# A hybrid decoder layer on one core: the order of the opening stage rearranged

## The chip, the core and the metric

The kernel runs on one core of a Trainium2 chip. TensorE (PE), VectorE (DVE), ScalarE (ACT), GpSimd (POOL) and SyncE (SP) each run their own instruction stream in order, and transfers run on 16 DMA engines beside them. The metric is the device time of one execution in microseconds (us); lower is better.

## The reference

One decoder layer for a sequence of 2048 rows of width 1024. Two attention mixers share one normalised, modulated input and one input projection:

```python
mod = jax.nn.silu(c) @ w_ada + b_ada
shift, scale, gate = jnp.split(mod, 3, axis=-1)
h = rms_norm(x, g_pre) * (1.0 + scale[:, None, :]) + shift[:, None, :]
proj = h @ w_in
qa, ka, va, fa, za, qb, kb, vb, zb = jnp.split(proj, split_points, axis=-1)
oa = forgetting_attention(qa, ka, va, fa + b_fgate)        # causal, 8 heads of 64
oa = oa * jax.nn.silu(za)
qb = rope(qb, positions); kb = rope(kb, positions)
ob = sliding_window_sink_attention(qb, kb, vb, sinks)      # window 128, 8 query heads, 2 key heads
ob = ob * jax.nn.silu(zb)
y = jnp.concatenate([oa, ob], axis=-1) @ w_out
x = x + gate[:, None, :] * rms_norm(y, g_post)
```

All inputs and the output are float32 in DRAM.

## The kernel before

Matrix products are made of three float16 products: each operand is split into a high and a low part. Rows are worked on in four chunks of 512 (`CH`); the model dimension is eight tiles of 128 (`KT`). Stages follow each other: the opening stage (lines 421 to 642), the sliding-window branch with the rest of the projections (1041 to 1105), the forgetting attention (1467 to 1555), and the output projection.

**The opening stage.** The rows of `w_ada` come as tiles `wa[half, k]` of 512 KB by `load_ada`; half 1 is `scale`, half 0 is `shift`. `mod` is a sum over the eight k: `ada_pe` lets PE multiply a tile by the broadcast silu(c), `ada_dve` accumulates a tile into `acc` on DVE, `ada_sum` lets PE add `acc` over the partitions, and `ada_col` brings the result from rows to columns. Between them DVE computes the rotary angles (`ang`, lines 510 to 541) from `posi` and `ifr`. x comes in tiles of 128 rows by `load_x`: tiles 0 to 3 and 8 to 11 go through four buffers of the pool `xin`, tiles 4 to 7 lie in the memory of `hT[3]`, tiles 12 to 15 in the pool `xlate`. `squares(ci)` (ACT, line 372) sums the squares of the four tiles of chunk `ci`, `root(ci)` (DVE, 92 to 106, thirteen small instructions) gives the reciprocal root, `normal(ci)` (382 on ACT, 384 on DVE) multiplies the rows by it.

The columns of scale and shift together with a bound on h give `Gp` and `Shp` (624, 625). `turn(ci, k)` transposes one 128-column tile of a chunk on PE (390); its `scaled` applies `Gp` and `Shp` on ACT (396), and its `split` makes the high and low halves of h^T on DVE (400, 401). The weights of kb, vb and zb0 are loaded by `w_load`, and then take `w_scale` (small DVE steps), `w_high` (ACT, 245) and `w_low` (DVE, 251). Their largest elements, which `w_scale` needs, are found by a reduce on DVE and spread over the partitions by PE (569 and 582 for kb and vb; `z_row` and `z_all`, 928 and 932, for zb0).

**The projection units.** After that, the work of PE is a list of units, `punits`, written out by hand. A unit is an eighth of one projection of one chunk (3 matmuls of 512 columns for kb and zb, 12 of 136 columns for vb): eight units for kb (307), eight for vb (740) and eight for zb0 (307) in each of the chunks 0 to 2, with the eight turns of the next chunk put between them at the places in `at_`. `fill` goes through the list; before unit n it calls what `events[n]` holds (`at_slice`), and `tick2` runs what `after(n, f)` has put off by n ticks, one tick every second unit. Other weights go through the same seven steps at fixed distances ahead of their first unit (the `lead` numbers in `add`): a fetch, a reduce, a store and a broadcast through DRAM on POOL's queue, scale, high, low. `spread(g)` copies the cosines and sines to all heads by SP's queue, and `gates` handles the forget gates, with the prefix sums in `sums`.

Within each of the two blocks that call `tc.manual_schedule()` every engine's instructions keep the written order; the two blocks themselves are merged when the program is built (`z_row`'s reduce on DVE, of the second block, runs ahead of `root(1)`, of the first). At run time no order changes.

Line 205 issues `w_load`'s transfers, 365 those of `load_x`, 435 those of `load_ada`, 415 and 416 those of `spread`.

## Time and profile before

| | |
|---|---|
| median of three runs | 1220.21 us (1219.88 to 1220.71) |
| the profiled execution | 1225.81 us, of which its trace spans 1224.0 us |
| mean granted clock of PE | 0.984 |
| busy in the span: PE, DVE, ACT, POOL | 1164.7, 908.5, 674.1, 141.5 us |
| instructions: PE, DVE, ACT, POOL | 10832, 2268, 1117, 252 |

Times inside the text are microseconds from the start of the trace's span. Rows of the timeline give start, duration, engine, line, operation, output and inputs, shapes and count; the bracket gives the idle time of the engine just before and what ended it. `PEld` is PE's weight load, `SPq` and `POOLq` are the instructions that issue transfers.

### The profile page before, as it was taken

To read this page: it belongs to the slowest core of one execution; us is meant where nothing else is said; L and a number is where in the kernel's file an instruction comes from. 1 tells how busy PE (TensorE), PEld (TensorE's weight loads), DVE (VectorE), ACT (ScalarE), POOL (GpSimd) and SP (SyncE) were. 2 spreads that over 40 slices of the span, in tenths; PEclk is the share of its full clock that TensorE was granted. 3 is DMA by queue.
4 is the path that set the end of the run, shared out by engine and by line. 5 is a ranking of instruction groups with operands and counts; after the bars stand their busy time and mean duration, and the time that the engine had idled before them with its cause. 6 is when DMAs were issued, how large, how long until landed. Compare 5 with 4: busy or idle time off the path is not lost.

```text
span 1224.0 us, 27391 instructions
## 1 busy us (share of the span) xinstructions
PE 1164.7 (95%) x10832; PEld 696.0 (57%) x10832; DVE 908.5 (74%) x2268; ACT 674.1 (55%) x1117; POOL 141.5 (12%) x252
## 2 busy tenths in 40 slices
PE   6789999999999998999999999999999979999996
PEld 2457546865558965555555555555555545555553
DVE  6866568586776646688888798878978788676665
ACT  2666445454655541576667666666766769433231
POOL 2011133223232210001010110010000000000000
PEclk9899999999999999999999999999999989999999
DMA  9554332324223322313344323122111146446652
GB/s 324 187 145 138 83 93 75 84 62 103 86 76 80 54 60 44 79 51 92 73 69 77 92 60 77 40 71 48 38 46 42 41 134 193 139 157 192 193 171 84
DMA packets 88180, 120.97 MB, mean 99 GB/s; under 512 B 27852, under 2 KB 63732, under 8 KB 88052
## 3 DMA queue, kind: packets, MB, share of 16 engines
q1 hardware_dynamic: 77076, 86.20, 23.9%
q0 software_dynamic: 10976, 33.03, 11.7%
q8 instruction: 85, 1.39, 0.6%
q14 instruction: 43, 0.35, 0.1%
HBM read 71.82 MB, written 25.18 MB: 79 GB/s over the span
## 4 chain that ended last, share of the span: by engine, by line
PE 78%; DVE 8%; DMA 6%; issue 3%; ACT 3%; SPq 2%; POOL 1%; DVEq 0%; ACTq 0%; POOLq 0%
PE bk L307 29%; PE bk L1405 13%; PE bk L325 7%; PE sta L1256 5%; PE sta L1257 4%; PE bk L1207 4%; PE poa L1282 2%; PE poa L1283 2%; PE poa L1280 2%; PE pxb L864 2%; PE pss L831 2%; PE pob L883 2%; PE bk L1368 1%; DVE pha L1270 1%; DMA hT<-in_x_dram 1%
## 5 line engine op out<-in xcount | busy, mean ns | idle before, releaser
L1263 ACT ACTIVATE p<-sta,lift,scl_qk 128x1024 f32<-128x1024 f32 (+2 forms) x160 | 171.8, 1074 | 132.2 <-PE sta L1257 75.7
L307 PE MATMUL bk<-hT,wh_qk 128*128 128x512 f16 x768 | 196.2, 381 | 0.4 <-DVE a_m L1210 0.4
L1405 PE MATMUL bk<-wohl,oz 128*128 128x512 f16 x768 | 172.1, 379 | 0.0
L1270 DVE TENSOR_TENSOR pha<-p,pha 128x1024 f16<-128x1024 f32 (+2 forms) x160 | 169.2, 1057 | 0.2 <-ACT pha L1267 0.2
L1210 DVE TENSOR_REDUCE a_m<-bk 128x1 f32<-128x512 f32 x192 | 130.4, 686 | 52.3 <-PE bk L1207 51.6
L1267 ACT ACTIVATE pha<-p 128x1024 f16<-128x1024 f32 (+2 forms) x160 | 148.0, 925 | 5.7 <-PE bk L307 0.5
L1405 PEld LDWEIGHTS <-oz 128*128 128x128 f16 x768 | 74.5, 99 | 81.2 <-DVE oz L1392 0.3
L1256 PE MATMUL sta<-T 128*128 128x512 f16 (+1 forms) x320 | 112.3, 351 | 7.4 <-ACT p L1263 7.3
L1280 PE MATMUL poa<-vt,pha 128*128 128x65 f16 x1088 | 117.7, 194 | 1.0 <-DVE ona L1289 1.0
L1283 PE MATMUL poa<-vt,pha 128*128 128x65 f16 x1088 | 117.3, 193 | 1.1 <-DVE pha L1270 1.0
L1282 PE MATMUL poa<-vt,pha 128*128 128x64 f16 x1088 | 117.7, 195 | 0.0
L307 PEld LDWEIGHTS <-wh_qk 128*128 128x128 f16 x768 | 72.7, 98 | 76.2 <-issue 2.9
L1207 PE MATMUL bk<-T 66*128 66x512 f16 (+2 forms) x320 | 110.5, 352 | 3.5 <-DMA T<-stq 3.1
L1280 PEld LDWEIGHTS <-pha 128*128 128x128 f16 x1088 | 102.3, 97 | 15.9 <-DVE ona L1289 2.4
L1257 PE MATMUL sta<-T 69*128 69x512 f16 (+1 forms) x320 | 111.1, 352 | 0.0
L1282 PEld LDWEIGHTS <-pha 128*128 128x128 f16 x1088 | 101.7, 98 | 11.6 <-issue 0.2
L1283 PEld LDWEIGHTS <-pha 128*128 128x128 f16 x1088 | 101.6, 99 | 1.3 <-DVE pha L1270 1.3
L307 PE MATMUL bk<-hT,wh_za 128*128 128x512 f16 x384 | 99.8, 378 | 0.0
L325 PE MATMUL bk<-wh_va,hT 128*128 128x128 f16 x1536 | 91.0, 219 | 1.3 <-issue 1.3
L325 PEld LDWEIGHTS <-hT 128*128 128x128 f16 x1536 | 87.4, 98 | 6.4 <-issue 3.8
L307 PE MATMUL bk<-hT,wh_zb 128*128 128x512 f16 x384 | 89.9, 379 | 1.1 <-DVE wh_zb L251 1.1
L307 PE MATMUL bk<-hT,wh_qb 128*128 128x512 f16 x384 | 87.2, 379 | 0.0
(491 smaller groups left out, 1885.2 us busy)
## 6 DMA issues: line engine op xcount, KB each, us to landing
wa<-in_w_ada_dram SPq DMA_DIRECT2D x16, 512.0 KB
z_d<-tz POOLq DMA_DIRECT2D x32, 256.0 KB, 3.9
T<-stq SPq DMA_DIRECT2D x128, 64.0 KB
T<-o_d SPq DMA_DIRECT2D x16, 512.0 KB
T<-z_d SPq DMA_DIRECT2D x16, 512.0 KB
xr<-in_x_dram SPq DMA_DIRECT2D x16, 512.0 KB
out_dram<-yg SPq DMA_DIRECT2D x15, 512.0 KB
xt<-in_x_dram SPq DMA_DIRECT2D x12, 512.0 KB
```

The source lines that it names most:

```text
L307: PE.matmul(ps, whl[:, a, k, :], hT[ci][:, b, k, :], start=(k == 0 and n == 0), stop=(k == KT - 1 and n == 2))
L325: PE.matmul(ps[:, u * P:(u + 1) * P], hT[ci][:, a, k, u * P:(u + 1) * P], whl[:, b, k, :], start=(k == 0 and n == 0), stop=(k == KT - 1 an ...
L1207: PE.matmul(mx[:, :w], T[0:XM, 0, i * P:(i + 1) * P], T[0:XM, 2, pc * CH:pc * CH + w], start=True, stop=True)
L1256: PE.matmul(self.st[:, o:o + w], T[:, 3, kb_], T[:, 1, qc], start=True, stop=False)
L1257: PE.matmul(self.st[:, o:o + w], T[0:XR, 2, kb_], T[0:XR, 0, qc], start=False, stop=not diag)
L1263: A.activation(self.p32[:, :self.w], self.st[:, :self.w], AF.Exp, scale=scl[f"qk{self.hd}"][:], bias=lift[:])
L1267: A.activation(self.ph[:, 0, :self.w], self.p32[:, :self.w], AF.Copy)
L1270: V.tensor_tensor(self.ph[:, 1, :self.w], self.p32[:, :self.w], self.ph[:, 0, :self.w], op=ALU.subtract)
L1280: PE.matmul(po[:, u, :], ph[:, 0, pq], vt[:, b, hd, 0:65], start=(self.first and n == 0 and u == 0), stop=False)
L1282: PE.matmul(po[:, u, 0:64], ph[:, 0, pq], vt[:, b, hd, 65:VW], start=False, stop=False)
L1283: PE.matmul(po[:, u, :], ph[:, 1, pq], vt[:, b, hd, 0:65], start=False, stop=(self.last and n == len(self.blocks) - 1))
L1405: PE.matmul(py, self.hl[:, i, k, :], w_slot(8 * j + k)[:, cc], start=(k == 0 and m_ == 0), stop=(k == KT - 1 and m_ == 2))
```

## The change

- The positions and `ifr` are loaded by ScalarE's queue, `ifr` first; SP then issues the eight tiles of scale's half of `w_ada` one after the other.
- The early fetch of zb0 on GpSimd's queue goes; the later one by SP stays and follows x 4 to 7.
- The two partial sums `ada_dve(0, 4)` and `(0, 6)`, and root(0) and normal(0), come after the scales of kb and vb; PE's last `ada_pe(0, 7)` goes ahead of the closing sum.
- `w_high("vb")` moves ahead of normal(0), `w_low` of kb and vb and the reduce over zb0 move later.
- normal(1) runs on DVE alone.
- x 8 to 11 are loaded at the end of the opening stage, x 12 to 15 at unit 1.
- squares, root and normal of chunks 2 and 3 come one chunk earlier; the turns lie at other units.
- zb0's steps move among units 10 to 16; the later weights' last steps are one unit earlier; `sums` is three ticks later.

```diff
--- before.py
+++ after.py
@@ -378,7 +378,7 @@
     def normal(ci, us=range(4)):
         for u in us:
             t, r = ci * 4 + u, rstd[ci][1][:, u:u + 1]
-            if ci == 0 or (ci == 1 and u % 2):
+            if ci == 0:
                 A.activation(xt[t], xt[t], AF.Copy, scale=r)
             else:
                 V.tensor_scalar(xt[t], xt[t], r, None, op0=ALU.mult)
@@ -434,16 +434,14 @@
             wa[half, k] = wad.tile([P, D], F32, tag="wa", name=f"wa{half}{k}")
             SP.dma_start(wa[half, k][:], w_ada0[k * P:(k + 1) * P, half * D:(half + 1) * D])
 
-        for k in range(1):
-            load_ada(1, k)
-
+
+        A.dma_start(ifr[:], inv_freq)
         for g in range(4):
-            SP.dma_start(posi[32 * g:32 * g + 32, :], positions[0, g * CH:(g + 1) * CH].partition_broadcast(32))
-        SP.dma_start(ifr[:], inv_freq)
-        for k in range(1, KT):
+            A.dma_start(posi[32 * g:32 * g + 32, :], positions[0, g * CH:(g + 1) * CH].partition_broadcast(32))
+        for k in range(KT):
             load_ada(1, k)
         make_identity(nc, ident)
-        for key in first:
+        for key in first[:2]:
             w_load(key, pieces(key))
         G.dma_start(snk[:], sinks[0].partition_broadcast(P))
         G.dma_start(bfg[:], b_fgate[0].partition_broadcast(P))
@@ -556,53 +554,50 @@
             load_x(t)
         for k in range(3, KT):
             load_ada(0, k)
-        w_load("zb0", pieces("zb0"), SP)
         for t in range(4, 8):
             load_x(t)
+        w_load("zb0", pieces("zb0"), SP)
         ada_sum(1, True)
 
         mx3 = st.tile([P, 2], F32, name="mx3")
         for n, key in enumerate(first[:2]):
             V.tensor_reduce(mx3[:, n:n + 1], wq[key][0][:], axis=AX.XY, op=ALU.max, apply_absolute_value=True)
+        PE.transpose(bk[0][0:2, 0:P], mx3[:], ident[:])
         ada_pe(0, 0, True)
-        ada_pe(0, 3)
-        PE.transpose(bk[0][0:2, 0:P], mx3[:], ident[:])
-        ada_pe(0, 5)
         ada_dve(0, 1, True)
         ada_dve(0, 2, False)
-        squares(0)
-        scl0 = col8("scl0")
-        ada_col(1, scl0)
-        root(0)
-        normal(0)
         m3 = st.tile([2, 1], F32, name="m3")
         V.tensor_reduce(m3[:], bk[0][0:2, 0:P], axis=AX.X, op=ALU.max)
         dg3 = st.tile([2, 2], F32, name="dg3")
         V.tensor_scalar(dg3[:], ident[0:2, 0:2], m3[:], None, op0=ALU.mult)
         PE.matmul(bk[0][:, P:P + 2], ones[0:2, :], dg3[:], start=True, stop=True)
-        ada_dve(0, 4, False)
-        ada_dve(0, 6, False)
-
-        for n in range(2):
-            nn = slice(n * CH, (n + 1) * CH)
-            PE.matmul(pm[0][n][:], ones[:], acc[0][:, nn], start=False, stop=False)
-            PE.matmul(pm[0][n][:], silb[:, KT - 1, :], wa[0, KT - 1][:, nn], start=False, stop=True)
+        ada_pe(0, 3)
+        ada_pe(0, 5)
+        squares(0)
+        scl0 = col8("scl0")
+        ada_col(1, scl0)
         V.tensor_copy(mxs[:, 0:2], bk[0][:, P:P + 2])
         for n, key in enumerate(first[:2]):
             wq[key].append(mxs[:, n:n + 1])
         w_scale("kb")
+        w_scale("vb")
         w_high("kb")
-        w_scale("vb")
-        w_low("kb", 0, 1)
+        w_high("vb")
         scl1 = col8("scl1")
         V.tensor_tensor(scl1[:], scl0[:], cols[:, 24:32], op=ALU.add)
         gcol = col8("gcol")
         V.scalar_tensor_tensor(gcol[:], scl1[:], 1.0, cols[:, 8:16], op0=ALU.add, op1=ALU.mult)
         absg = col8("absg")
         V.scalar_tensor_tensor(absg[:], gcol[:], -1.0, gcol[:], op0=ALU.mult, op1=ALU.max)
+        root(0)
+        normal(0)
+        ada_dve(0, 4, False)
+        ada_dve(0, 6, False)
+        ada_pe(0, KT - 1)
+        ada_sum(0, True)
+        w_low("kb", 0, 1)
         turned = [turn(0, k) for k in range(5)]
         squares(1)
-        w_high("vb")
         shf0 = col8("shf0")
         ada_col(0, shf0)
         shf = col8("shf")
@@ -625,17 +620,19 @@
         V.tensor_scalar(Shp[:], shf[:], ipH[:], 2.0 ** 14, op0=ALU.mult, op1=ALU.mult)
 
         V.tensor_scalar(pfl[:], ipH[:], 0.5, None, op0=ALU.mult)
-        w_low("vb", 0, 1)
         for k in range(KT):
             turned[k][0]()
             turned[k][1]()
             if k == 2:
-                V.tensor_reduce(mxs[:, 2:3], wq["zb0"][0][:], axis=AX.XY, op=ALU.max, apply_absolute_value=True)
+                w_low("vb", 0, 1)
             if k + 5 < KT:
                 turned.append(turn(0, k + 5))
         root(1)
+        V.tensor_reduce(mxs[:, 2:3], wq["zb0"][0][:], axis=AX.XY, op=ALU.max, apply_absolute_value=True)
         normal(1)
         spread(0)
+        for t in range(8, 12):
+            load_x(t)
         for key in ("kb", "vb"):
             kaps[key] = kappa(pws[key], key)
         V.tensor_scalar(kf[:], kaps["vb"][:], PS_SCALE, None, op0=ALU.mult)
@@ -800,7 +797,7 @@
 
         after(1, logs)
         after(3, total)
-        after(4, sums)
+        after(7, sums)
 
     ab = {}
 
@@ -902,11 +899,11 @@
             at = len(punits) - (24 if key[:2] == "za" else 0)
             for n, (lead, f) in enumerate(((42, lambda: w_load(key, pieces(key))), (31, lambda: w_max(key)),
                                            (21, lambda: w_back(key)), (12, lambda: w_scale(key)),
-                                           (8, lambda: w_high(key)), (6, lambda: w_low(key, 0)),
-                                           (4, lambda: w_low(key, 1)), (3, lambda: w_done(key)))):
+                                           (9, lambda: w_high(key)), (7, lambda: w_low(key, 0)),
+                                           (5, lambda: w_low(key, 1)), (4, lambda: w_done(key)))):
                 if key == "zb0":
                     if n >= 3:
-                        events.setdefault(n + 9, []).append(f)
+                        events.setdefault((13, 13, 14, 15, 16)[n - 3], []).append(f)
                 else:
                     events.setdefault(max(at - lead, n), []).append(f)
         if key not in pkeys:
@@ -933,8 +930,9 @@
         V.tensor_copy(mxs[:, 2:3], bk[2][:, P:P + 1])
         wq["zb0"].append(mxs[:, 2:3])
 
-    at_slice(6, z_row)
-    at_slice(10, z_all)
+    at_slice(10, z_row)
+    at_slice(12, z_all)
+    at_slice(1, lambda: [load_x(t) for t in range(12, 16)])
 
     for ci in range(NCH):
         n0 = len(punits)
@@ -944,19 +942,18 @@
             add(*others[ci])
 
             mine, punits[n0:] = punits[n0:], []
-            at_ = [10, 12, 14, 16, 17, 18, 19, 20] if ci else [12, 14, 16, 17, 18, 19, 20, 21]
+            at_ = [6, 8, 10, 12, 14, 16, 18, 20] if ci else [13, 15, 17, 18, 19, 20, 21, 22]
             for n, u in enumerate(mine):
                 punits.append(u)
                 if n in at_:
                     punits.append(lambda ci=ci, k=at_.index(n): turn_x(ci + 1, k))
-            if ci:
+            if ci < 2:
+
                 for u in range(4):
-                    at_slice(n0 - 9 + 2 * u, lambda ci=ci, u=u: squares(ci + 1, (u,)))
-                    at_slice(n0 + 3 + u, lambda ci=ci, u=u: normal(ci + 1, (u,)))
-                at_slice(n0 + 2, lambda ci=ci: root(ci + 1))
+                    at_slice(n0 + (3 if ci else 9) + u, lambda ci=ci, u=u: squares(ci + 2, (u,)))
+                    at_slice(len(punits) - 6 + u, lambda ci=ci, u=u: normal(ci + 2, (u,)))
+                at_slice(len(punits) - 9, lambda ci=ci: root(ci + 2))
             at_slice(n0 + 12, lambda ci=ci: spread(ci + 1))
-            if ci < 2:
-                at_slice(n0 + 12, lambda ci=ci: [load_x(t) for t in range(4 * ci + 8, 4 * ci + 12)])
     n0 = len(punits)
     at_slice(n0, lambda: open_fox())
     at_slice(n0 + 8, gates)
```

## The prediction

> **What bounds the kernel now.** I read the page first, then busy time by stretch (columns: stretch and its length, then busy time and count for PE, PEld, DVE, ACT, POOL, then granted clock, DMA share, GB/s).
>
> ```profile
> PE 1164.7 (95%) x10832; PEld 696.0 (57%) x10832; DVE 908.5 (74%) x2268; ACT 674.1 (55%) x1117; POOL 141.5 (12%) x252
> ...
> 58.40:81.30 22.90, 20.66 (x178) 14.30 (x178) 15.79 (x49) 18.59 (x30) 1.27 (x1) 1.00 0.52 150
> ...
> 103.00:126.50 23.50, 21.80 (x176) 15.61 (x175) 17.86 (x43) 14.11 (x26) 3.61 (x5) 0.93 0.36 90
> ...
> 160.00:300.00 140.00, 140.00 (x1424) 89.15 (x1423) 99.47 (x278) 76.81 (x215) 41.88 (x79) 1.00 0.33 83
> ```
>
> PE is busy 95% of the span, and from 160 to 300 us it has no gap (140.00 of 140.00). The instruction order per engine is fixed at build time, so whatever arrives earlier at 160 us arrives earlier at the end. The change is therefore priced in the first 160 us, where PE has gaps. There are two parts: the adaLN stage, which ends when h^T's factors `Gp`, `Shp` are known, and projection chunks 0 to 2 (kb, vb, zb0 on 512 rows each, with the next chunk's h^T turns between them).
>
> **Term 1: when h^T can start.** Timeline rows (start, duration, what, idle before):
>
> ```profile
> 4.36 0.88 POOL L205 DMA_DIRECT2D wr_zb<-in_w_in_dram  x1
> ...
> 13.38 0.49 DVE L514 TENSOR_SCALAR ang<-ang,ifr 128x512 f32<-128x512 f32 x1 [1.28 <-DMA ifr<-in_freq_dram]
> ...
> 22.24 0.75 DVE L478 TENSOR_SCALAR acc<-wa,sil 128x1024 f32<-128x1024 f32 x1
> ...
> 28.51 0.39 SPq L205 DMA_DIRECT2D wr_zb<-in_w_in_dram  x1
> ...
> 32.26 0.17 DVE L92 TENSOR_SCALAR rs_v<-ss 128x4 f32<-128x4 f32 x1 [1.00 <-ACT junk L372]
> 32.32 0.50 PEld L471 LDWEIGHTS bk<-wa,silb 128*128 128x128 f32 x2 [4.51 <-DMA wa<-in_w_ada_dram]
> ...
> 34.64 4.27 ACT L382 ACTIVATE xt<-xt,rst 128x1024 f32<-128x1024 f32 x4 [2.42 <-DVE rst L106]
> ...
> 35.78 1.88 PE L471 MATMUL bk<-wa,silb 128*128 128x512 f32 x4
> ...
> 36.43 2.59 DVE L480 SCALAR_TENSOR_TENSOR acc<-wa,sil,acc 128x1024 f32<-128x1024 f32 x2
> ...
> 42.75 0.68 DVE L490 TENSOR_TENSOR acc<-bk,ident 128x512 f32<-128x512 f32 x1
> ...
> 48.68 0.76 ACT L396 ACTIVATE hT<-px,Shp,Gp 128x512 f16<-128x512 f32 x1
> ...
> 63.72 1.14 ACT L245 ACTIVATE wh_zb<-wr_zb,w_sw 128x1024 f16<-128x1024 f32 x1
> ...
> 20.00:25.00 5.00, 5.00 (x13) 2.17 (x12) 4.86 (x7) 2.18 (x5) 0.00 (x0) 1.00 1.03 410
> ```
>
> The stage is fed at a full DMA rate of 410 GB/s (last row). The weight `zb0` is fetched twice (4.36 and 28.51). The early one goes: 0.5 MB at 410 GB/s is 1.25 us by which x and the last rows of w_ada land sooner. x 4 to 7 also pass the remaining zb0 fetch, another 1.25 us, but chunk 1 alone uses them.
>
> Root(0) waits for x (32.26, released by ACT's squares), so it starts at about 31.0 and its 2.38 us (32.26 to 34.64) end at 33.4. In the new DVE order the two partial sums of 2.59 us follow at once, without the 36.43 start: they end at 36.0. Row 7 of w_ada lands meanwhile: w_ada's second half reaches k=3 at 32.32, four more rows at 1.25 us make 37.3, less 1.25 is 36.1. Its matmuls (1.88) end at 38.0 and the closing sum (1.88) at 39.8. Before, both products came after the partial sums and DVE read them at 42.75. From there to the first h^T at 48.68 are 5.93 us of short DVE and PE steps. I take 0.2 off, for `w_high("vb")`, which now leaves ACT earlier. So T, the first h^T activation, moves from 48.68 to 45.6: **3.1 us gained**. w_low("kb") goes ahead of those steps on DVE, under the closing sum's 1.88 us; without that cover it costs 1.3, half of the 2.59. On ACT the high parts of kb and vb, two like the 1.14 of wh_zb's, now stand between the squares (31.0) and normal(0): they end at 33.3, when the root does, so they cost nothing.
>
> Positions go to ScalarE's queue. Its five issues stand ahead of ACT's first activation, where ACT had to wait anyway. The angle chain starts at ifr's landing (13.38) and ends at 22.24, 8.9 us of DVE. No row shows ACT's queue; landing anywhere between the start and 13.38 is possible. I take 8, with little effect: the partial sums behind it end early enough for root(0) to wait for x, not for DVE. If positions land as late as before, all DVE steps behind them slip (ada_col(1), the scales, root(0)); I put that at 1.7 us, the part of the 3.1 that no DMA row secures, and T gains 1.4. At the other end, the early fetch may have taken twice its share of the rate, which is 1.25 more. Bounds 1.4 to 4.4.
>
> **Term 2: chunk 0 and its end.** What is moved into it, and what it costs on DVE and ACT:
>
> ```profile
> 52.75 1.21 DVE L633 TENSOR_REDUCE mxs<-wr_zb 128x1 f32<-128x1024 f32 x1
> ...
> 59.10 0.60 ACT L697 ACTIVATE qf<-bk 128x512 f32<-128x512 f32 x1 [2.31 <-PE bk L307]
> ...
> 61.32 2.19 ACT L382 ACTIVATE hT<-hT,rst 128x1024 f32<-128x1024 f32 x2 [1.62 <-DVE rst L106]
> 61.32 1.42 DVE L384 TENSOR_SCALAR hT<-hT,rst 128x1024 f32<-128x1024 f32 x2
> ...
> 64.90 1.49 DVE L251 SCALAR_TENSOR_TENSOR wh_zb<-wr_zb,w_sw,wh_zb 128x512 f16<-128x512 f32 x2 [0.41 <-ACT wh_zb L245]
> ...
> 66.30 0.81 PE L307 MATMUL bk<-hT,wh_zb 128*128 128x512 f16 x3
> ...
> 67.86 1.98 SPq L365 DMA_DIRECT2D xt<-in_x_dram  x4
> ...
> 78.26 1.06 ACT L372 ACTIVATE junk<-xt 128x1024 bf16<-128x1024 f32 x1
> ...
> 74.70:82.00 7.30, 5.30 (x27) 2.29 (x26) 3.26 (x6) 7.27 (x13) 0.00 (x0) 1.00 0.42 115
> ...
> 82.72 0.16 DVE L92 TENSOR_SCALAR rs_v<-ss 128x4 f32<-128x4 f32 x1
> ...
> 85.10 3.75 DVE L384 TENSOR_SCALAR xt<-xt,rst 128x1024 f32<-128x1024 f32 x4
> ```
>
> Up to T+9.7 (58.4) DVE's and ACT's work is as before, and kb(0) ends at T+10.4 (59.10). From 58.4 to 81.3, when the last split of chunk 1's h^T ends, DVE was busy 15.79 of 22.90 us and ACT 18.59; at the end ACT is full (7.27 of 7.30) and kb of chunk 1 starves beside it: 5.30 busy. ACT loses two normals (2.19), and the four squares of x 8 to 11 start sooner, so ACT is no longer last. DVE gains two normals (1.42), the zb0 reduce (1.21, from before 58.4 to behind root(1)), root(2) (82.72 to 85.10, 2.38) and normal(2) (4 at 0.71, half of 1.42, 2.84): 7.9 us. DVE would need 15.8 + 7.9 = 23.7 of the 22.9 us, and full only if it never waits; with 1.3 us of waits it needs 25. So kb(1), which ended at 82.0 (T+33.3), would end at T+9.7+25 = T+34.7, and 0.3 for the last matmuls: T+35. **1.7 us lost.** PE also waits at `z_row`, now slice 10, for the reduce behind root(1), some 2 us; that lies under the DVE bound. If PE alone bounded, kb(1) would end at T+31 (below), a gain of 2.2; if DVE waits 3 us more, a loss of 4.
>
> **Term 3: chunks 1 and 2.** Their PE gaps:
>
> ```profile
> 63.72 1.58 PE L740 MATMUL bk<-wh_vb,hT 128*128 128x136 f16 x24
> ...
> 82.00:89.20 7.20, 3.57 (x40) 2.58 (x38) 6.70 (x19) 0.57 (x2) 1.94 (x2) 0.82 0.43 117
> ...
> 86.00 0.30 PE L390 MATMUL px<-ident,xt 128*128 128x128 f32 x1 [1.95 <-DVE xt L384]
> ...
> 86.00:90.00 4.00, 2.32 (x12) 1.48 (x13) 3.44 (x4) 0.58 (x1) 1.36 (x1) 0.58 0.45 107
> ...
> 89.17 2.93 PE L740 MATMUL bk<-wh_vb,hT 128*128 128x136 f16 x24
> ...
> 120.19 0.44 PE px L390 x4
> ...
> 126.75 5.34 PE L307 MATMUL bk<-hT,wh_kb 128*128 128x512 f16 x24
> ...
> 131.93 5.84 PE L740 MATMUL bk<-wh_vb,hT 128*128 128x136 f16 x96
> ```
>
> In both chunks root and normal stand where PE needs the turned rows at once (82.0 to 89.2: PE 3.57 of 7.20; for chunk 2 inside its 21.80 of 23.50, at a clock of 0.93). The change puts them one chunk earlier, so this wait goes. A chunk without waits is kb 5.34, vb 5.84, zb 5.34, eight turns at 0.44: 20.0. Chunk 1 from kb's end took 21.0 (82.0 to 103.0); now 14.7, with 0.4 of friction 15.1: **5.9 gained**. Chunk 2 took 23.5; now 20.4: **3.1 gained**. Next late would be DVE, which carries 17.86 in a 23.5 us chunk, root and normal among it; that is under 20.4, so PE stays last. By the same parts, PE from T+10.4 to kb(1)'s end is 5.84 + 5.34 + 3.5 + 5.34, the T+31 above.
>
> The clock: 24 vb matmuls took 2.93 at 89.17 and 1.58 at 63.72, with a granted clock of 0.58 in 86 to 90, behind PE idle times of at most 1.95. The Trainium skill (TensorE: Matmul & The Clock Gate, HAM oscillation) says that the clock is halved by PE-idle gaps over about 3.4 us; here it fell without one, so the measurement decides. By that rule nothing falls in the new chunk 1; by the rows a half-starved PE can fall. The nearest case is 74.7 to 82.0, starved and granted 1.00, so I add nothing; the other end is 1.7 us lost.
>
> **Term 4: later.**
>
> ```profile
> 108.94 0.91 POOL L205 DMA_DIRECT2D wr_qb<-in_w_in_dram  x1
> ...
> 137.60 5.34 PE L307 MATMUL bk<-hT,wh_qb 128*128 128x512 f16 x24
> ...
> 148.68 0.46 PE L781 MATMUL bk<-nf,triu 128*128 128x128 f32 x2 [0.55 <-DVE nf L776]
> ...
> 156.07 2.33 PE L307 MATMUL bk<-hT,wh_zb 128*128 128x512 f16 x10 [1.10 <-DVE wh_zb L251]
> ```
>
> `sums` three ticks later removes 0.55; weight parts one slice sooner may remove up to 1.10. Against it, qb0's weight takes 28.7 us from fetch to use (108.94 to 137.60), and the 42 slices between now take 26 of 32 parts of chunk 2's 20.4, and kb and vb of chunk 3 (5.34 + 5.84): 27.8, up to 0.9 lost. Sum **0.5 gained**, from 1.6 gained to 3.5 lost, if qb0's and zb1's fetches, which both begin in chunk 2, hand back its 3.1 and these 0.9. In all later weights only the slice of ACT's and DVE's parts moves; their work is the same: 0.
>
> **Sum.** 3.1 - 1.7 + 5.9 + 3.1 + 0.5 = 10.9 us. The profiled execution (1225.81, span 1224.0) would be 1214.9. The three timed runs have the median 1220.21, 5.6 below the profiled one; against it the time is **1209.3**.
>
> **Rivals.** *DVE finds room.* Root(2) and normal(2) come in DVE's waits, and kb(1) ends with PE at T+31, 3.9 more: 1205.4. For it: DVE had 7.1 us free in 58.4 to 81.3. Against: their place is ahead of the last splits.
>
> *Fetches bite.* qb0's and zb1's chains run at DMA speed, not PE's, and give 4 us back: term 4 is at its lower end, -3.5, and the time 1213.3. For it: the slack is nil by the rows above; against: PE has none of these waits at 137.60.
>
> *Positions land no sooner.* T gains 1.4: 1211.0. For it: the DMA engines were full at 20 to 25 and positions still cross the same stage. This is what the Trainium skill (DMA: Bandwidth & Descriptors, Issuing engines are not separate DMA queues) makes of it: a second issuing engine saves only issue time. No run here shows it yet.
>
> *Squares wait for x (slower).* Four squares of x 8 to 11 now stand on ACT ahead of wh_zb. Behind x 11's landing come a square (1.06), wh_zb (1.14) and its low part (1.49), 3.7 us, and then zb0 on PE. That began at 66.30 (T+17.6) and should begin at T+19.6 with `z_row`'s wait. A landing later than T+26.8 loses the whole gain (19.6 + 10.9 - 3.7). If SP issued those loads no sooner than before (67.86, T+19.2), and the last again needed 10.4 to its square (78.26), zb0 would start at T+33.3, 13.7 us late: 1223.0. Against it: the slots of x 0 to 3 come free with chunk 0's last turn, ahead of T+9.7, and even 10.4 from there is T+20.1.
>
> **How the numbers follow.** Forecast 0.37, DVE finds room 0.25, fetches bite 0.17, positions no sooner 0.12, squares wait 0.07, and 0.02 that gains and losses meet within 0.2% (2.4 us, about what a measurement of this kernel can tell). Faster 0.91, same 0.02, slower 0.07. The range goes from 1203.0 (DVE finds room, with term 1's upper end, 1.3, and term 4's, 1.1) to 1216.0 (fetches bite, with term 2's worst end, 2.3 more, and 0.4 of the clock).
>
> **What would show it.** First h^T activation at 45 to 46; one zb0 fetch; squares of x 8 to 11 before wh_zb; DVE over 90% busy until kb(1) ends near 80; no PE gap over 1 us in chunks 1 and 2; qb0 at about 127. It is wrong if the first h^T stays at 48, if ACT idles at a square for x, or if PE waits for DVE in chunk 1 again.

## The result and the profile after

The changed kernel is slower: 1226.5 us (median of 5 runs) against 1220.2 us for the kernel before, ratio 1.0046 with a 95% interval of 1.0035 to 1.0057. The forecast was 1209.3, 0.9% faster. Its profiled execution took 1227.15 us (span 1225.2).

The page of the kernel after, and then busy time by stretch, with the columns of the prediction; the first stretch runs from 9.7 us after the first h^T activation (58.40 in the prediction's table) to the end of chunk 1's kb product, called kb(1):

```profile
PE 1166.2 (95%) x10832; PEld 696.4 (57%) x10832; DVE 908.1 (74%) x2270; ACT 672.7 (55%) x1115; POOL 140.4 (11%) x251
...
55.70:82.50 26.80, 24.00 (x185) 17.85 (x185) 24.44 (x71) 19.91 (x32) 1.33 (x1) 0.87 0.49 161
...
127.00:160.00 33.00, 27.06 (x153) 13.16 (x151) 16.71 (x59) 10.60 (x21) 5.94 (x9) 0.90 0.31 77
...
600.00:800.00 200.00, 196.53 (x1967) 110.97 (x1966) 169.85 (x363) 127.92 (x150) 17.15 (x27) 1.00 0.31 68
```

Sums over the whole span say nothing: PE has the same work. By stretch there are two places. In 127 to 160 us PE is idle 5.9 of 33.0 us (before: 1.7). And in 600 to 800 us, which no step of the prediction looked at, it is idle 3.5 of 200 us (before: 0.4).

The opening came out as forecast. Timeline of the kernel after (start, duration, what, idle before):

```profile
8.77 0.43 DVE L511 CAST ang<-posi 128x512 f32<-128x512 int32 x1 [2.51 <-DMA posi<-in_positions_dram]
...
45.97 0.78 ACT L396 ACTIVATE hT<-px,Shp,Gp 128x512 f16<-128x512 f32 x1 [2.71 <-DVE pfl L622]
...
59.85 0.27 PE L925 MATMUL bk<-ident,mxs 128*1 128x128 f32 x1 [1.99 <-DVE mxs L631]
59.96 2.56 PE L737 MATMUL bk<-wh_vb,hT 128*128 128x136 f16 x24
...
130.93 5.34 PE L307 MATMUL bk<-hT,wh_qb 128*128 128x512 f16 x24 [1.69 <-DVE qc L699]
...
151.32 5.01 PE L307 MATMUL bk<-hT,wh_zb 128*128 128x512 f16 x12 [4.25 <-DVE tz L347]
...
156.26 0.67 PE L828 MATMUL pss<-kst,stb 64*128 64x128 f16 x12
```

The first h^T activation is at 45.97 (45.6 forecast), kb(3) ends at 123.6 (before: 132.1). Then qb0, forecast at 127, begins at 130.93, zb1 waits 4.25 us and runs at about half the clock (granted 0.54 in 151.3 to 156.3; 5.01 us for 12 matmuls, 2.75 with the full clock), and the scores (L828) begin at 156.26, only 2.1 us ahead of the 158.33 of before.

What stands behind zb1's wait, the longer of the two, is on ScalarE, and begins at kb(3)'s end (qb0's wait comes with the experiments). Kernel after, ACT, POOL and DVE:

```profile
126.08 0.29 DVE L230 TENSOR_REDUCE w_mx<-mxr 128x1 f32<-128x128 f32 x1 [4.28 <-DMA mxr<-mx_d]
...
126.97 0.15 DVE L237 TENSOR_SCALAR w_sw<-w_sw 128x1 f32<-128x1 f32 x1
...
127.21 1.15 ACT L245 ACTIVATE wh_qb<-wr_qb,w_sw 128x1024 f16<-128x1024 f32 x1 [7.29 <-PE bk L737]
128.27 0.58 ACT L694 ACTIVATE qf<-bk 128x512 f32<-128x512 f32 x1
...
138.34 1.26 POOL L708 TENSOR_TENSOR qs<-qs,sinT 128x512 f32<-128x512 f32 x1 [7.23 <-DMA qs<-qf]
139.64 0.69 DVE L709 TENSOR_TENSOR qc<-qc,qs 128x512 f32<-128x512 f32 x1 [6.33 <-POOL qs L708]
...
140.37 0.63 ACT L710 ACTIVATE stb<-qc 128x512 f16<-128x512 f32 x1 [10.65 <-DVE qc L709]
140.90 0.58 ACT L694 ACTIVATE qf<-bk 128x512 f32<-128x512 f32 x1
...
149.98 0.69 DVE L709 TENSOR_TENSOR qc<-qc,qs 128x512 f32<-128x512 f32 x1 [4.01 <-POOL qs L708]
150.59 0.68 DVE L347 SCALAR_TENSOR_TENSOR tz<-tz,bk 128x512 f32<-128x512 f32 x1
```

With the new leads the high part of qb0 (L245) stands on ACT ahead of the copy of kb's finished product (L694). It needs the scale `w_sw`, which waits for a DMA (L230, 4.28 us) and was done only at 126.97 + 0.15 = 127.12. So ACT stood still for 7.29 us, the last 3.6 of them with kb's product lying ready from 123.6. (The row puts the wait down to PE; the scale is what ended last, and with the old leads the same wait is put down to it.) The rotary chain starts from that copy: DMA, POOL's product (L708), DVE's sum (L709, 139.64). ACT waits 10.65 us for that sum (L710), so the copy of qb0's product behind it runs only at 140.90. Its own sum is at 149.98 on DVE, and L347, for which zb1 waits, stands behind it at 150.59. The Trainium skill (PSUM — Partial Sum Buffer, Engine vs sequencer instructions) says that the queues of ScalarE, VectorE and GpSimdE are strictly first in, first out. The trace agrees: the copy, ready at 123.6, ran on ACT at 128.27, behind L245.

### The profile page after: what moved, and what is told of

It is laid out like the page before. It is cut to its first block, busy times and chain, and to the rows that moved or that the text cites. A ratio compares the mean times of both kernels' runs of the same rounds, so it can differ in the third digit from the quotient of the medians.

```text
span 1225.2 us, 27384 instructions
## 1 busy us (share of the span) xinstructions
PE 1166.2 (95%) x10832; PEld 696.4 (57%) x10832; DVE 908.1 (74%) x2270; ACT 672.7 (55%) x1115; POOL 140.4 (11%) x251
## 3 DMA queue, kind: packets, MB, share of 16 engines
q8 instruction: 85, 1.39, 0.5%
## 4 chain that ended last, share of the span: by engine, by line
PE 74%; DVE 9%; DMA 7%; issue 5%; ACT 3%; POOL 1%; SPq 1%; DVEq 0%; ACTq 0%; POOLq 0%
PE bk L307 26%; PE bk L1402 13%; PE bk L325 6%; PE sta L1253 5%; PE sta L1254 4%; PE bk L1204 4%; PE poa L1279 2%; PE poa L1280 2%; PE poa L1277 2%; DMA wa<-in_w_ada_dram 2%; PE pxb L861 2%; PE pob L880 1%; DMA qs<-qf 1%; PE pss L828 1%; DVE a_m L1207 1%
## 5 line engine op out<-in xcount | busy, mean ns | idle before, releaser
L1253 PE MATMUL sta<-T 128*128 128x512 f16 (+1 forms) x320 | 113.0, 353 | 10.7 <-ACT p L1260 10.6
```

The costliest lines, as they stand in the source:

```text
L1253: PE.matmul(self.st[:, o:o + w], T[:, 3, kb_], T[:, 1, qc], start=True, stop=False)
```

## The experiments

The theories at the start: A, the lead won by chunk 3 is handed back at qb0 and zb1 because their fetch chains run at their own speed; B, the leads of the later weights cost time in the attention stages; C, the profiled execution of before was unlike its timed runs, and the gaps that were priced were in part its own. Later ones are named where they come up.

All kernels were timed beside the kernel before; intervals are of 95%. Leads are quoted as high, first low, second low, done, in slices (units of the list) ahead of the weight's first use: (8, 6, 4, 3) in the kernel before, (9, 7, 5, 4) in the kernel after. The code cuts are shortened: `(8, high)` stands for `(8, lambda: w_high(key))`, and so on.

**The kernel before, again.** Diff: none.

> The kernel before, unchanged, for a second profiled execution of it. The profiled execution on which the prediction stood took 1225.81 us (span 1224.0), 5.6 us above the timed runs' 1220.21. Theory C (that execution was slower than the timed ones in some stretch): a new profile has a span near 1218.5 and shows where the 5.6 us lie; if they lie in the first 160 us, the gaps that the prediction priced were partly peculiar to that execution. Theory A or B (the lead is handed back, or lost later): the first 160 us of the new profile are the same within 1 us (qb0's first matmul at 137.6, first scores at 158.3), and the span differs behind that.

1220.9 us, ratio 1.0006 (0.9995 to 1.0017); profiled at 1219.39, span 1217.6. The execution on which the prediction stood was 6.4 us longer in span than this one of the same program. The timelines differ by at most 0.5 us up to 115 us and by 1.6 at the scores; the rest lies later, for instance where the forgetting attention waits for its first transposed scores' operand. Before, and in the second fence before again:

```profile
465.00 0.22 PE L1207 MATMUL bk<-T 66*128 66x128 f16 x1 [3.08 <-DMA T<-stq]
...
466.09 1.49 PE L307 MATMUL bk<-hT,wh_qk 128*128 128x512 f16 x3
```

```profile
460.96 0.22 PE L1207 MATMUL bk<-T 66*128 66x128 f16 x1 [2.00 <-DMA T<-stq]
461.02 0.81 PE L307 MATMUL bk<-hT,wh_qk 128*128 128x512 f16 x3
```

The gaps that the prediction priced were for the most part not peculiar to that execution: from kb(1)'s end to kb(3)'s it took 50.2 us, this one 49.0. Theory C explains 5.6 us between a profile and the timed runs, and at most 1.2 us of the miss.

**The leads alone, on the kernel before, and undone in the kernel after.** 

```
-  (8, high) (6, low 0) (4, low 1) (3, done)
+  (9, high) (7, low 0) (5, low 1) (4, done)
```

> The kernel before, with only the leads of all weights' parts changed to those of the change (9, 7, 5, 4 slices for high, the two lows and done, in place of 8, 6, 4, 3). Theory B (these leads cost time in the attention stages, where ACT and DVE work in order): slower than before by 3 to 6 us, 1223 to 1226, the loss behind 450 us. Theory A (all is lost by fetch chains ahead of 160 us): the same as before within 1 us, 1220. The prediction's own term for this was 0.

> The kernel after, with the old leads 8, 6, 4, 3 for all weights' parts but zb0's. Theory B: faster than after by 3 to 6 us, 1220 to 1223, the lead of some 2.5 us at 160 us kept to the end. Theory A: as after within 1 us, 1226, or slower by up to 1 where the later lows hold up zb1 further.

On the kernel before the new leads alone cost: 1229.58 us, ratio 1.0071 (1.0056 to 1.0087), 8.7 us. The kernel after with the old leads takes 1213.59 us, ratio 0.9944 (0.9929 to 0.996): 6.9 us **faster** than before, and 12.4 faster than the kernel after by the ratios (1.0046 less 0.9944, of 1220.5). That is well over the 3 to 6 us that theory B had expected. Theory A, in which the fetch chains alone take the lead back, falls: with the old leads the same fetches are in time. The same place on ACT, POOL and DVE, then PE, in the kernel after with the old leads:

```profile
121.60 0.60 ACT L694 ACTIVATE qf<-bk 128x512 f32<-128x512 f32 x1 [3.69 <-PE bk L307]
124.40 1.15 ACT L245 ACTIVATE wh_qb<-wr_qb,w_sw 128x1024 f16<-128x1024 f32 x1 [2.21 <-DVE w_sw L237]
...
127.21 1.53 POOL L708 TENSOR_TENSOR qs<-qs,sinT 128x512 f32<-128x512 f32 x1
...
131.15 0.69 DVE L709 TENSOR_TENSOR qc<-qc,qs 128x512 f32<-128x512 f32 x1
...
127.08 5.51 PE L307 MATMUL bk<-hT,wh_qb 128*128 128x512 f16 x24
...
144.19 3.00 PE L307 MATMUL bk<-hT,wh_zb 128*128 128x512 f16 x12 [0.80 <-DVE tz L347]
147.12 0.67 PE L828 MATMUL pss<-kst,stb 64*128 64x128 f16 x12
```

The copy leaves ACT at kb's end, the wait for the scale comes behind it, POOL's product is 11.1 us earlier, qb0 begins at 127.08 (forecast: about 127), and the scores 9.1 us ahead of the kernel after (2.0 of them were there at kb(3)'s end, so 7.1 arise here).

The fetch chain still has a part in it. On the kernel before the new leads put the same two activations in the same order:

```profile
130.97 1.15 ACT L245 ACTIVATE wh_qb<-wr_qb,w_sw 128x1024 f16<-128x1024 f32 x1 [4.49 <-PE bk L307]
132.03 0.58 ACT L697 ACTIVATE qf<-bk 128x512 f32<-128x512 f32 x1
```

There kb(3) ends at 130.9 and the scale is done at 130.26, so the copy is only 1.1 us late and the scores begin at 156.98 (before again 156.74): nothing is lost at this place, and the 8.7 us all come later. In the kernel after, the opening and the chunk moves bring kb(3)'s end forward to 123.6, ahead of the scale at 127.12. The loss here needs both, the early high part and the earlier chunk 3.

**sums.** 

```
-        after(7, sums)
+        after(4, sums)
```

> The kernel after, with sums back at tick 4 of the forgetting gates' chain (7 in the change). If the later sums are what delays the scores and the decay behind them: faster by 1 to 3 us, 1223 to 1225. If sums only fill a wait, as the prediction had it: slower by 0.5, 1227. Theories A and B both expect a difference of under 1 us.

1226.5 us, 1.005 (1.0033 to 1.0066): no difference. The 0.55 us that the prediction gave to it can't be measured in this kernel.

**High part or low parts.** The kernel after with (9, 6, 3, 3), and with (8, 7, 5, 4). The first was meant to have (6, 4, 3) behind the 9, as its expectation says; its second low part stands one slice later than that:

```
-  (9, high) (7, low 0) (5, low 1) (4, done)
+  (9, high) (6, low 0) (3, low 1) (3, done)      first kernel
+  (8, high) (7, low 0) (5, low 1) (4, done)      second kernel
```

> The kernel after with only the high part one slice early (9) and the lows and done at their old leads (6, 4, 3). The old leads throughout gave 1213.6, the change's leads 1226.5: 12.9 us to place. Theory H (it is the high part: at 9 slices ACT reaches it before the evacuation copy of the projection that ends there, and stands waiting for the weight's factor or for the one q/k buffer that PE still reads, with the copy behind it): 1224 to 1227, nearly all of the 12.9 us. Theory L (it is the low parts on DVE, ahead of the rotary steps): 1213 to 1216.

> The kernel after with only the lows and done one slice early (7, 5, 4) and the high part at its old lead 8. Theory H: 1213 to 1215, as with all old leads. Theory L: 1224 to 1227. If the two share it, this and the kernel with only the high part early add up to 12.9 us over 1213.6.

With the high part alone early: 1224.51 us, 1.0025 (1.0014 to 1.0037), 9.9 us above the old leads by the ratios. With the low parts alone early: 1214.84, 0.9948 (0.9932 to 0.9963), 0.5 above. Theory L falls. No wait of PE for a low part shows in the first kernel, so its late second low isn't seen to cost anything. The two add up to 10.4 of the 12.4; the 2 us between are within the four intervals together, and are left open.

The two traces also part the two waits of PE. qb0 with the high part alone early, then with the low parts alone early:

```profile
127.41 5.45 PE L307 MATMUL bk<-hT,wh_qb 128*128 128x512 f16 x24
```

```profile
130.52 5.34 PE L307 MATMUL bk<-hT,wh_qb 128*128 128x512 f16 x24 [1.69 <-DVE qc L699]
```

zb1's wait is 3.96 us in the first and under 0.5 in the second. So qb0's wait of 1.69 us in the kernel after doesn't come from the high part: it stands there with the high part behind the copy, in a kernel that is as fast as the old leads within 0.5 us.

**Which high parts.** First the q weights at the old lead, then qb0's alone:

```
-  (9, lambda: w_high(key))
+  (8 if key[0] == "q" else 9, lambda: w_high(key))      first kernel
+  (8 if key == "qb0" else 9, lambda: w_high(key))       second kernel
```

> The kernel after with the change's leads, but the high part of the q weights (qb0 to qb3, qk0 to qk7, whose split tiles share one buffer with kb's) at the old lead 8; va, za and zb weights (two buffers) keep 9. Theory H1 (the wait for the single buffer, and the copy of a q or k projection behind it): 1213 to 1217, the wait of wh_qk for PE (10.7 us in 6 waits in the profile after) and the 6 us wait of DVE for the rotary product near 135 us gone. Theory H2 (any high part ahead of any copy costs): the q weights are 12 of the 25, so half is left, near 1220.

> The kernel after with the high part of qb0 alone at the old lead 8 and all other leads as changed. The loss of 12.9 us has two places in the traces: 7 us by the scores' begin at 150 us (qb0's high part ahead of kb's last rotary copy), 5 us in the forgetting attention (wh_qk waits for PE to finish with its single buffer, 10.7 us in 6 waits). If that reading is right: 1219 to 1221, scores near 149, and the wh_qk waits stay at 10.7. If the later q weights' place alone decides: 1225.

With all q weights at 8: 1216.79 us, 0.996 (0.9944 to 0.9975), so the q weights carry 10.5 of the 12.4 us; theory H2 (any high part) would have left half. With qb0 alone at 8: 1220.91, 0.9999 (0.999 to 1.0008), so this one activation costs 5.7 us in the kernel after; the scores begin at 148.38. What is left shows in the groups of ACT (after the second bar: idle time just before them, and for whom). The wh_qk group of the kernel after, of after with the old leads, and of after with only qb0 at 8:

```profile
L245 ACT ACTIVATE wh_qk<-wr_qk,w_sw 128x1024 f16<-128x1024 f32 x8 | 9.2, 1148 | 14.0 <-PE bk L307 10.7 <-DVE w_sw L237 3.4
```

```profile
L245 ACT ACTIVATE wh_qk<-wr_qk,w_sw 128x1024 f16<-128x1024 f32 x8 | 9.1, 1141 | 1.8 <-PE bk L307 1.0 <-DVE w_sw L237 0.8
```

```profile
L245 ACT ACTIVATE wh_qk<-wr_qk,w_sw 128x1024 f16<-128x1024 f32 x8 | 9.2, 1149 | 13.3 <-PE bk L307 10.7 <-DVE w_sw L237 2.6
```

ACT stands 10.7 us for PE with a qk weight's high part, in 6 waits, when it is a slice early, and 1.0 us with the old leads. The pool `wpq` has one buffer for the split weights of kb, qb and qk. At 8 slices the weight that sat in it has had its last matmul; at 9 that last slice is still to come, and ACT waits for it, with the exponentials that PE needs queued behind. The waits of PE name them (total in us, times, longest), in the kernel after and with the old leads:

```profile
PE sta L1253 <- ACT p L1260: 10.6, 9, 4.2
```

```profile
PE sta L1253 <- ACT p L1260: 7.2, 5, 5.2
```

**A second buffer.** Whether the wait for the buffer costs, or the place ahead of the exponentials, is told apart by a buffer of its own for qk3, qk5 and qk7; room for it comes from a staging buffer, taken away in the control as well.

```
-    stp = ... tile_pool(name="stpa", bufs=3, ...)
+    stp = ... tile_pool(name="stpa", bufs=2, ...)                both kernels
+    fx["wpk"] = fox_pool("wpk", 1, side="right")                 second kernel
-    pool = ... wpq if key[0] in "qk" else wpool
+    pool = ... fx["wpk"] if key in ("qk3", "qk5", "qk7") else wpq if key[0] in "qk" else wpool
```

> The kernel after with two staging buffers in place of three in the forgetting attention (2 KB less), nothing else: the control for the next kernel, which needs that room. If the third buffer is seldom used: 1226.5 within 1. If it is: slower by some us; in either case the next kernel is compared with this one.

> As the control before it, with a buffer of their own for the split weights of qk3, qk5 and qk7, so that from qk3 on no high part writes the buffer that PE still reads. The order of the instructions on ACT stays. Buffer theory (the wait of wh_qk for PE, 10.7 us in 6 waits, holds back the exponentials): the waits of qk3 to qk7 go, and 3 to 5 us with them. Order theory (the high part's place ahead of the copy and the exponentials costs by itself): as the control within 1 us.

The control takes 1226.28 us, 1.0039 (1.0026 to 1.0052); with the second buffer 1221.25, 1.0002 (0.9992 to 1.0013). The high parts of one weight, qk5, in the control and with the buffer:

```profile
733.09 1.15 ACT L245 ACTIVATE wh_qk<-wr_qk,w_sw 128x1024 f16<-128x1024 f32 x1 [2.75 <-PE bk L307]
...
735.18 1.19 ACT L1260 ACTIVATE p<-sta,lift,scl_qk 128x1024 f32<-128x1024 f32 x1
736.27 0.58 ACT L993 ACTIVATE stq<-bk 128x512 f16<-128x512 f32 x1
```

```profile
726.27 1.15 ACT L245 ACTIVATE wh_qk<-wr_qk,w_sw 128x1024 f16<-128x1024 f32 x1 [0.45 <-DVE w_sw L237]
...
728.36 1.19 ACT L1261 ACTIVATE p<-sta,lift,scl_qk 128x1024 f32<-128x1024 f32 x1
729.45 0.58 ACT L993 ACTIVATE stq<-bk 128x512 f16<-128x512 f32 x1
```

The order on ACT is the same, the wait is 0.45 in place of 2.75 and for another thing (over all eight weights the wait for PE falls from 10.7 to 1.1), and 4.5 us are gone by the ratios. The buffer theory holds, the order theory falls for this stage. Not all 4.5 is certain to be the buffer's: the two profiled executions also differ by 2.7 us at 450 to 480 us, at the wait for the first `T`; from 500 us to the end the kernel with the buffer gains 4.4.

**The qk weights alone, on the kernel before.**

```
-  (8, lambda: w_high(key))
+  (9 if key[:2] == "qk" else 8, lambda: w_high(key))
```

> The kernel before with the high part of the eight qk weights alone one slice early (9 for 8), nothing else changed. If the single buffer is what costs in the forgetting attention: 4 to 7 us slower than before, 1225 to 1228, with steps of about 1 us at each qk weight between 430 and 900 us, and 160 us reached as before. If the loss needs the early lows too: within 1 us of before.

1224.91 us, 1.0031 (1.0019 to 1.0043): 3.8 us from one slice on eight activations, a little under the 4 to 7 expected. wh_qk again waits 10.7 us for PE, and against the kernel before again the timeline falls back in steps of 0.4 to 1.0 us, at four of the qk weights (3, 4, 5 and 7), 3.2 us in all between 590 and 880 us.

**The opening alone, and the chunk moves alone**, each put on the kernel before with the old leads and `sums` as before. Of the change's diff the two take these parts:

```
first kernel: every hunk up to `turned = [turn(0, k) for k in range(5)]`, w_high("vb") among them, without normal()
+        A.dma_start(posi[...], positions[...])
+        for key in first[:2]:
...
+        ada_sum(0, True)
second kernel: normal(), and every hunk behind that line but sums and leads
+            if ci == 0:
+        for t in range(8, 12):
+            load_x(t)
...
+    at_slice(10, z_row)
+                at_slice(len(punits) - 9, lambda ci=ci: root(ci + 2))
```

> The kernel before with the opening stage of the change alone (positions on ScalarE's queue, one zb0 fetch, x 4 to 7 sooner, the new order up to the first h^T); chunk moves, sums and leads as before. The prediction's term 1 makes 3.1 us of it (1.4 to 4.4): 1217.1. If the lead is kept to the end: first h^T near 45.5, time 1216 to 1218. If fetch chains take it back (the rival that fetches bite): first h^T near 45.5 but qb0 at 136 as before, and 1220.

> The kernel before with the moves in chunks 0 to 2 alone (squares, roots, normals and turns of the next chunk, x loads, zb0's maximum and parts, z_row and z_all later); opening stage, sums and leads as before. The prediction's terms 2 and 3 make 7.3 us of it (-1.7 + 5.9 + 3.1): 1213. If the two parts add up to the 6.9 us measured with the old leads: 3 to 4 us faster, 1216 to 1217. If this part is worth nothing and the opening all: 1220.

The opening: 1217.83 us, 0.9976 (0.9966 to 0.9987), 2.9 us faster; term 1 had 3.1. Its qb0 begins at 131.03 and nothing is handed back there. In the profiles its lead over before again is 4.8 us at the first h^T, 5.8 at the scores and 2.8 at the end, so that 2.9 so near 3.1 is partly luck. The chunk moves: 1218.51, 0.9979 (0.9971 to 0.9988), 2.6 us faster where terms 2 and 3 had 7.3. What became of the rest is in its timeline:

```profile
62.49 0.27 PE L930 MATMUL bk<-ident,mxs 128*1 128x128 f32 x1 [1.99 <-DVE mxs L636]
...
65.57 0.58 PE L934 MATMUL bk<-mz,ones 1*128 1x1 f32 x2 [1.16 <-DVE kf L643]
66.41 2.88 PE L742 MATMUL bk<-wh_vb,hT 128*128 128x136 f16 x24 [0.25 <-DVE mxs L935]
...
133.75 5.59 PE L307 MATMUL bk<-hT,wh_qb 128*128 128x512 f16 x24 [1.62 <-DVE qc L704]
...
147.07 0.46 PE L783 MATMUL bk<-nf,triu 128*128 128x128 f32 x2 [2.55 <-DVE nf L778]
```

kb(1) ends at 85.7 (82.0 before): 3.7 lost, where 1.7 was forecast and 4 was the bound. Chunks 1 and 2 then gain 8.2 (from kb(1)'s end to kb(3)'s 40.8 us, before again 49.0), 4.5 ahead at kb(3)'s end; qb0 and the gates' sum wait 1.62 and 2.55 us, and the scores begin 1.3 us ahead: 3.2 handed back, near the 4 of the rival that fetches bite. But only in part for its reason. The 2.55 are a wait for DVE's `nf`, not for a fetch, in a kernel with `sums` at its old tick; with `sums` three ticks later, in the kernel after and with the old leads, no such wait is left.

**VectorE in chunk 0.** Two kernels, both with the old leads: the zb0 maximum ahead of the root, and half of chunk 1's normalisations back on ACT.

```
-        root(1)
         V.tensor_reduce(mxs[:, 2:3], wq["zb0"][0][:], ...)
+        root(1)                                                first kernel
-            if ci == 0:
+            if ci == 0 or (ci == 1 and u % 2):                 second kernel
```

> The kernel after with the old leads for all weights, and the zb0 maximum on DVE ahead of root(1) in place of behind it. Before this, z_row stood on PE for 1.99 us waiting for that maximum, and z_all 1.39 us. If DVE bounds chunk 0's end, as the prediction's term 2 had it (the same DVE work, in another order): 1213.6 within 1. If PE's wait is on the path: z_row's 2 us go, z_all's wait grows by up to 1.2, and it is 1 to 2 us faster, 1211.6 to 1212.6.

> The kernel after with the old leads, and with two of the four normalisations of chunk 1 given back to ScalarE, as before the change (1.42 us off VectorE, 2.19 us onto ScalarE). If VectorE is what holds chunk 0's end (term 2): z_all's and zb0's waits fall by up to 1.4, and the time is 1212 to 1213 (old leads alone: 1213.6). If ScalarE is then the later one, as it was before the change: 1213.6 to 1215.

The first takes 1214.22 us, 0.9942 (0.9924 to 0.996), as the old leads alone (0.9944). Its z_row and z_all on PE, and behind them those of the old leads alone:

```profile
57.74 0.27 PE L925 MATMUL bk<-ident,mxs 128*1 128x128 f32 x1
...
63.09 1.99 PE L737 MATMUL bk<-wh_vb,hT 128*128 128x136 f16 x24 [3.35 <-DVE mxs L930]
```

```profile
58.31 0.27 PE L925 MATMUL bk<-ident,mxs 128*1 128x128 f32 x1 [1.99 <-DVE mxs L631]
58.42 1.58 PE L737 MATMUL bk<-wh_vb,hT 128*128 128x136 f16 x24
61.39 0.38 PE L929 MATMUL bk<-mz,ones 1*128 1x1 f32 x2 [1.39 <-DVE kf L638]
```

The wait of 1.99 goes and that of 1.39 becomes 3.35: VectorE has the same work ahead of the last of them, so PE merely waits at another place, and kb(1) ends 36.2 us after the first h^T in both. VectorE is the bound there, as term 2 said. The second kernel takes 1214.28 us, 0.9947 (0.9934 to 0.9959): z_all's wait is gone as expected, but the clock fell in that execution (24 vb matmuls 2.88 us, granted 0.50 in 61.8 to 64.5) and kb(1) ended no sooner. Whether taking work off VectorE pays is left open by it.

**The other way.** The kernel after with (7, 5, 4, 3):

```
-  (9, high) (7, low 0) (5, low 1) (4, done)
+  (7, high) (5, low 0) (4, low 1) (3, done)
```

> The kernel after with the leads moved the other way: high at 7, lows at 5 and 4, done at 3 (old: 8, 6, 4, 3). If the order on ACT decides, nothing more is won, since at 8 the high part already stands behind the copy: 1213.6 within 1. If earlier is simply worse by the slice, it goes on: 1209 to 1212. If the high part now comes late for its lows: slower, 1215 to 1220.

1214.24 us, 0.9947 (0.9934 to 0.9959), as with 8. So it is not that every slice earlier costs: between 9 and 8 the high part passes the copy and the last reader of its buffer, and between 8 and 7 it passes nothing that can be measured. The kernel after with the old leads is the fastest of the set, at 1213.59 us.

## Why the prediction was wrong

Times in us of the profiled executions; the two columns of before are its two executions, "kb" is the end of a chunk's kb product.

| | before | before again | forecast | after, old leads | after |
|---|---|---|---|---|---|
| first h^T (T) | 48.68 | 49.05 | 45.6 | 44.42 | 45.97 |
| kb(1) less T | 33.2 | 33.0 | 35.0 | 36.2 | 36.7 |
| kb(3) less kb(1) | 50.2 | 49.0 | 9.0 less | 40.9 | 40.9 |
| qb0 begins | 137.60 | 136.49 | 127 | 127.08 | 130.93 |
| scores begin | 158.33 | 156.74 | | 147.12 | 156.26 |
| forgetting attention begins | 488.99 | 483.26 | | 476.44 | 486.00 |
| span | 1224.0 | 1217.6 | | 1210.6 | 1225.2 |

**The step that failed** is the last sentence of term 4: in all later weights only the slice of ACT's and DVE's parts moves, their work is the same: 0. It was 12.4 us of loss (8.7 when the leads alone are changed on the kernel before). The work is indeed the same, but the sentence priced work and not places: it named neither what is queued behind the high part on ACT nor who uses the one buffer that it writes. 5.7 us of it are qb0's high part ahead of kb's copy, a loss that arises only with the earlier chunk 3 of the same change; some 4 are the eight qk weights' wait for the buffer, which the kernel before loses as well (3.8 of its 8.7). The remaining 2.7, and 4.9 of the 8.7, are not taken apart further.

**What else was off** makes 4 of the remaining us: 10.9 were forecast with the leads at 0, 6.9 measured with the old leads.

Term 1 was right in kind and a little small: the first h^T comes at 44.1 to 46.0 in the profiled executions with the new opening and at 48.4 to 49.1 in those without, 3.7 us on the mean (3.1 forecast). Positions were read at 8.77 on DVE (forecast 8; before 11.68). The rival that they land no sooner falls in this case: the positions were issued 1.8 us sooner (the last at 3.20 on ScalarE's queue, 5.04 on SyncE's before) and landed 2.9 sooner. It drew on the Trainium skill (DMA: Bandwidth & Descriptors, Issuing engines are not separate DMA queues), by which a second issuing engine saves only issue time. Whether the 1.1 us beyond the issue time go against that isn't shown, since the change also takes away the early zb0 fetch, which the prediction put at 1.25.

Term 2 was too small: kb(1) came 3.0 to 3.2 later after T, not 1.7. With the old leads VectorE was busy 24.3 us of the 26.5 from 9.7 us after T to kb(1)'s end, where the term had 23.7 of 25: a little more work, and more waits. Term 3 was right: 8.0 to 9.2 in the two chunks, 9.0 forecast. That qb0 is at 127.08 with the old leads, as forecast, is partly luck: T was 1.2 us sooner than forecast in that execution, and kb(1) less T 1.2 more.

The rest went behind. The kernel after with the old leads is 9.6 us ahead of before again at the scores and 6.8 at the start of the forgetting attention, and that stays to the end (7.0). The prediction had looked for gaps only up to 300 us; its statement that what is earlier at 160 us is earlier at the end was right for two thirds. The lead, 10.0 us at 445 us, is 6.8 at 477: these 3.2 us go at the wait for the first `T` (3.53 us in place of 2.00) and in the slower matmuls behind it:

```profile
452.45 0.22 PE L1204 MATMUL bk<-T 66*128 66x128 f16 x1 [3.53 <-DMA T<-stq]
...
453.83 1.49 PE L307 MATMUL bk<-hT,wh_qk 128*128 128x512 f16 x3
```

The kernel before had 3.08 and 2.00 there in its two executions. Over all the profiled executions the wait is 1.74 to 3.08 us in the five with the old opening, four of them at most 2.09, and 2.70 to 4.08 in the thirteen with the new one. So most of it comes with the new opening; why it is longer there is not shown.

**The signs it named** were all there up to kb(3): one zb0 fetch, h^T at 45.97, squares of x 8 to 11 ahead of wh_zb without a wait for x (so the slower rival was not what happened), DVE busy 24.44 of 26.80 us until kb(1)'s end at 82.5 (forecast 80), no PE gap over 0.75 us in chunks 1 and 2. The one that failed was qb0 at 127 (130.93, with the 1.69 us of the early low parts). The range's lower and upper ends both assumed the later stages untouched, and no rival was made of the leads.

## What to carry to other kernels

An instruction that is only moved on an in-order queue costs by what it passes, not by its work: before moving it, list what stands behind it in the new place, when its own inputs are ready there, and who last reads the buffer that it writes. A part moved earlier by one step can cross the last reader of a single buffer, and then it turns from early work into a stall for its whole engine. Change such a parameter by itself: here a gain of 7 us and a loss of 12 came in one change, and only their sum showed. And try it on the new order too: on the kernel before, qb0's early high part lost nothing at its place.

## What the hardware showed beside that

The clock of PE fell behind idle pieces of unlike length, and not in each execution. Behind the same wait of 1.99 us, 24 vb matmuls took 2.56 us in the kernel after (granted clock 0.58 in 59.9 to 62.6) and 1.58 with the old leads (1.00 in 58.4 to 60.0). Behind 2.00 us at `T` 3 matmuls took 0.81 in before again (granted 1.00); behind 3.08 and 3.53 us they took 1.49 a little later (granted 0.50 in both). The Trainium skill (TensorE: Matmul & The Clock Gate, HAM oscillation) puts the limit at gaps of about 3.4 us. The fall behind 1.99 and 3.08 us doesn't fit that as a lower limit, and the measurement decides. So in these runs a wait of 2 us on PE cost about 1 us more or nothing. That is part of why two executions of one program lay 6.4 us apart: at `T` they parted by 1.1 us in the wait and by 1.7 more in the slower matmuls behind it.
